# A seven-product group for the second retention pair, with banks, transposes and input chunks rearranged around it

## The chip, the cores and the metric

The kernel runs on one core of one Trainium2 chip. Its engines work from queues of their own: TensorE (PE in the profile) multiplies matrices, VectorE (DVE), ScalarE (ACT) and GpSimd (POOL) work on tiles, and SyncE (SP) issues most of the loads. The metric is device time in microseconds (us) for one execution; lower is better. Before the change the median of three runs is 1776.27 us (1775.71 to 1776.57).

## The reference

Two layers of a decoder trunk over 512 tokens with 1024 features, in float32. One projection feeds two branches, retention and an mLSTM; their gated sum goes through an output projection, a layer norm, a SwiGLU block and a second norm.

```python
proj = x @ w_in[l]
(r_q, r_k, r_v, r_g, m_qk, m_v, m_o, m_i, m_f, g_a, g_b) = jnp.split(proj, IN_OFFSETS, axis=-1)
rq = _rotary(r_q...);  rk = _rotary(r_k...) * (RET_QK_DIM ** -0.5)
o_ret = _head_norm(_retention(rq, rk, rv), ret_norm_g[l]) * silu(r_g)
mq, mk = silu(causal_conv(m_qk)) ...
o_ml = _head_norm(_mlstm(mq, mk, mv, i_pre, f_pre), mlstm_norm_g[l]) * sigmoid(m_o)
mix = (sigmoid(g_a) * (o_ret @ w_ret) + sigmoid(g_b) * (o_ml @ w_ml)) @ w_out[l]
x = layer_norm(alpha * x + mix);  x = layer_norm(alpha * x + swiglu(x))
```

Each branch has four heads, with 128 features for queries and keys and 256 for values.

## The kernel before, in words

**Precision.** Each float32 operand of a large product is split into a high part of a reduced type (`hi`, a cast on ScalarE, line 201) and the low rest (`lo`, a subtraction on VectorE, line 133). Each product is then three matmuls: high by high, high by low, low by high.

**Weights.** All weights lie in one array of units of 128 x 1024 values (512 KB). `layer_plan` lists a layer's units in the order of use. SP loads them into five raw buffers; `hi_to` and `prep_to` make the parts, up to five units ahead of use and four asked for by `used`. TensorE and SP follow the order in which the program is written out. The other engines are ordered by a planner, except inside the seven-product groups, where ScalarE, VectorE and GpSimd follow the program as well.

**Ways of multiplying.** `feat` (lines 266 to 268) takes one unit and makes 128 features for all 512 tokens, 24 matmuls of 512 columns. `tok_units` (lines 360 to 362) makes, over four units, 512 features for four blocks of 128 tokens, each in its own PSUM bank: a stream. `quad` (line 324) takes four units at once as a 2 x 2 block product and does it with seven block products instead of eight, 168 matmuls of 256 columns. It needs sums of weight blocks (`sum_to` line 191 on VectorE, line 223 on GpSimd) and sums of input blocks, the tiles `xs`, which `input_sums` makes (adds on GpSimd, line 589, four additions on VectorE, line 595, a cast on ScalarE, line 596, a low part on VectorE). Before the change, the mLSTM's queries and keys, the merge gates and most of the SwiGLU projections are made by such groups. Which units they take stands in `QUADS`.

**Banks.** PSUM has eight banks: four main ones (`main_bank`, `pm`), for units and streams, and four auxiliary ones (`aux_bank`, `pa`), for the side work. A group uses four main banks and one auxiliary one.

**Stages around the change.** For each retention pair `p` of two heads: four query/key units with the rotary turn (`rot_evac`, lines 618 to 621), for the first pair the gate unit (`feat_if`, whose `if_evac` is a chain of small operations on the rows of the input and forget gates), then a value stream and a gate stream. Then each mLSTM pair: a group with a convolution, a value stream, a gate stream.

**Side work and places.** The work of the heads is written as generators in the queue `side`; `slot()` takes one step of the first one in it. `slot()` is called after each token block of a stream (16 places a stream), after every two k-steps of a unit (4 places), and twice per block product of a group (14). `rest(n)` is `n` empty steps. The generators: `scores` (3 steps: two halves of the scores, lines 468 and 469; then key transposes, line 478, from which ScalarE and VectorE make the weighted keys, lines 482 and 483), `if_cols` (transposes of the gate rows, line 671), `weighted` (5 steps: the state, then four token blocks, lines 494 to 496), and `head_norms` (15 steps with 16 transposes, line 550). At the end of a pair, `drain()` runs what is left in the queue. A second queue, `slow`, holds `input_sums`; every fifth call of `slot()` (`SLOW`) takes one step of it. It is filled when the second retention pair starts.

The order in `side` for the first retention pair is: `scores` of the first head, `rest(12)`, `if_cols`; and, once the value stream has been written out, `weighted` of the first head, `scores` of the second, `rest(2)`, `weighted` of the second.

**The start.** The input comes transposed in six chunks (four of one k-tile, two of two), the first four units in matching pieces on SP's queue. The first four chunks are issued from ScalarE's queue, the last two from SP's, between the pieces. Each chunk is split (lines 428 to 433) when it lands. `first_units` multiplies the first four k-tiles for all four units, then the rest unit by unit (lines 343 to 345).

Of the kernel before, what the change touches and what calls it, by code (L numbers as in the profile page):

```python
# [10 lines left out]
F32 = mybir.dt.float32  # L11
F32R = mybir.dt.float32r
AF = mybir.ActivationFunctionType
ALU = mybir.AluOpType
# [84 lines left out]
QUADS = [layer_plan().index(("F", w, c + j * P)) for w, c, js in (("in", O_MQK, (0, 2)), ("in", O_GA, (0, 4)),  # L99
# [5 lines left out]
def decoder_trunk(ctx: ExitStack, tc: tile.TileContext, wall, xT_in, x_in, pvec, lnp, rtab, out):  # L105
# [15 lines left out]
    def aux_bank():  # L121
        return psa.tile([P, 512], F32, tag="a", name="pa")

# [119 lines left out]
    SLOW = 5  # L243
    turn = {"n": 0}

    def slot():
        turn["n"] += 1
        if slow and turn["n"] % SLOW == 0:
            if next(slow[0], "end") == "end":
                slow.popleft()  # L250
# [169 lines left out]
    k0 = 0  # L420
    for n in (1, 1, 1, 1, 2, 2):
        t = scratch([P, n, S], "xraw")
        ks, cs = slice(k0, k0 + n), slice(k0 * P, (k0 + n) * P)
        (nc.scalar if n == 1 else nc.sync).dma_start(t, xT_in[:, ks, :])
        for i, (r, hi, lo) in enumerate(firsts):
            nc.sync.dma_start(r[:, cs], wall[i][:, cs])
        if k0 == 0:
            nc.vector.tensor_copy(xh[:, ks, :], t)
        else:
            nc.scalar.copy(xh[:, ks, :], t)  # L430
        lo_of(xl[:, ks, :], t, xh[:, ks, :])
        for r, hi, lo in firsts:
            nc.scalar.copy(hi[:, cs], r[:, cs])
            lo_of(lo[:, cs], r[:, cs], hi[:, cs])
        k0 += n
# [23 lines left out]
    def scores(qk, hh, box, mult, key_weight, query_weight):  # L459
# [16 lines left out]
        pa = aux_bank()  # L476
# [21 lines left out]
    def weighted(box, vh, vl, hh, nv, done):  # L498
# [4 lines left out]
        pa = aux_bank()  # L503
# [6 lines left out]
        for i in range(NB):  # L510
            c, e = i // 2, i % 2
            pa = aux_bank()
            w = [(0, e * P)] + ([(1, HC)] if e else [])
            for n, (j, o) in enumerate(w):
                three(pa[:, :nv], cut(2 * c * W1 + o, P, W1), val(2 * c + j), n == 0, c == 0 and n == e)
            if c:
                three(pa[:, :nv], cut(O_QD + e * P, P, HC), st, False, True)
            done(i, pa)
            yield

    def head_norms(oo, p, gt, gain, od):
# [22 lines left out]
        for hh in range(2):  # L544
            m = 2 * (2 * p + hh)
            t = scratch([P, 2, S], "ot")
            for f in range(2):
                pa = aux_bank()
# [55 lines left out]
    for l in range(L):  # L604
# [9 lines left out]

        def rot_evac(dst):
            def ev(pm):
                t = scratch([P, S], "rt")
                nc.vector.tensor_tensor(out=dst, in0=pm, in1=tab[:, 0], op=ALU.mult)
                nc.vector.tensor_tensor(out=t[0:64], in0=pm[64:128], in1=tab[0:64, 1], op=ALU.mult)
                nc.vector.tensor_tensor(out=t[64:128], in0=pm[0:64], in1=tab[64:128, 1], op=ALU.mult)  # L620
                nc.gpsimd.tensor_tensor(out=dst, in0=dst, in1=t, op=ALU.add)
            return ev
# [44 lines left out]
        def if_cols():  # L667
            r3 = rows[:, 3]
            pa = aux_bank()
# [6 lines left out]
        for p in range(2):  # L676
            if p == 1:
                slow.append(input_sums(xh, xl, *xs))
# [30 lines left out]
            if p == 0:  # L709
                side.append(rest(12))  # L710
# [9 lines left out]
            tok_units([main_bank() for _ in range(NB)], lambda k: xh[:, k], lambda k: xl[:, k], K8, True, True, v_evac)  # L720
# [37 lines left out]
        def conv_ev(qk):  # L758
            t = {}
            part = lambda i, h: qk[:, 2 * i : 2 * i + 2, h * HC : (h + 1) * HC]  # L760
            two = lambda bank: bank.rearrange("p (j t) -> p j t", j=2)

            def ev(name, banks):
                if name == "p1":
                    t["u"] = scratch([P, 2, 2, HC], "mu")
                    nc.scalar.copy(t["u"][:, 0], two(banks["a"]))
                elif name == "p5":
                    nc.scalar.copy(t["u"][:, 1], two(banks["c"]))
                elif name == "p7":
                    nc.vector.tensor_tensor(out=part(1, 1), in0=t["u"][:, 1], in1=two(banks["d"]), op=ALU.subtract)  # L770
                elif name == "p6":
                    u, v = t["u"][:, 0], t["u"][:, 1]
                    nc.vector.tensor_tensor(out=u, in0=two(banks["b"]), in1=u, op=ALU.add)
                    nc.gpsimd.tensor_tensor(out=v, in0=v, in1=u, op=ALU.subtract)
                    nc.gpsimd.tensor_tensor(out=part(1, 1), in0=part(1, 1), in1=u, op=ALU.subtract)
                elif name == "p2":
                    nc.scalar.copy(part(0, 0), two(banks["a"]))
                    nc.vector.tensor_tensor(out=part(1, 0), in0=two(banks["e"]), in1=t["u"][:, 1], op=ALU.add)
                elif name == "p4":
                    nc.vector.tensor_tensor(out=part(0, 1), in0=two(banks["d"]), in1=t["u"][:, 0], op=ALU.add)  # L780
            return ev

        for p in range(2):
            qk = reg.tile([P, 4, S], F32, tag="qk", name="mqk")
            with tc.manual_schedule(engines=ordered):
                quad(xh, xl, *xs, conv_ev(qk))
# [42 lines left out]
            tok_units([main_bank() for _ in range(NB)], lambda k: xh[:, k], lambda k: xl[:, k], K8, True, True, v_evac)  # L829
# [22 lines left out]
            tok_units([main_bank() for _ in range(NB)], lambda k: xh[:, k], lambda k: xl[:, k], K8, True, True, g_evac)  # L852
            drain()
            gain = pv[:, C_MG : C_MG + 8]
# [379 lines left out]
```

## Time and profile before

| what | value |
|---|---|
| median of three runs | 1776.27 us (1775.71 to 1776.57) |
| profiled execution, its own time | 1776.88 us |
| span of the profile | 1775.2 us |
| TensorE busy | 1760.3 us, 99% |
| VectorE busy | 1311.3 us, 74% |
| ScalarE busy | 793.9 us, 45% |
| GpSimd busy | 432.9 us, 24% |
| mean granted TensorE clock | 0.998 |

The span runs from the first to the last instruction; the profiled execution's own time lies 1.7 us above it. Matmuls are pipelined: one of 512 columns is shown as some 0.39 us long, but the next starts 0.23 us after it, so starts are to be compared, not lengths. A row of a table of stretches gives the stretch, its length, the busy time of TensorE, its weight loads, VectorE, ScalarE and GpSimd with the number of instructions in brackets, the granted clock, the busy share of the DMA engines and what they moved in GB/s. A row of the time line gives start, length, engine, line, operation, output and inputs, shapes and count, and in brackets the idle time ahead with what ended it.

### The profile page before, as it was taken

Reading aid. Unit: us, or ns where it says so; the run is one execution under the profiler, and the core shown is the slowest. Engines: PE = TensorE matmul, PEld = TensorE weight load, DVE = VectorE, ACT = ScalarE, POOL = GpSimd, SP = SyncE. Lnnn points to the kernel's source line nnn. Section 1 sums busy time; section 2 is a strip of 40 time slices with the busy share of each in tenths; the row PEclk is TensorE's granted clock in tenths of the full one; section 3 lists DMA queues with packets and bytes.
Section 4 is the critical chain, followed back from the end, with each engine's and each line's share of the span. In section 5 each row is a group of like instructions: output and inputs, shape, how many; then the busy total and the mean of one; then the engine's idle time right before and its main releaser. Section 6 shows DMA issues by size and latency. Waiting matters only on the chain.

```text
span 1775.2 us, 27167 instructions
## 1 busy us (share of the span) xinstructions
PE 1760.3 (99%) x10904; PEld 1586.0 (89%) x10904; DVE 1311.3 (74%) x1735; ACT 793.9 (45%) x1157; POOL 432.9 (24%) x321
## 2 busy tenths in 40 slices
PE   9999999999999999999999999999999999999997
PEld 7888898998889999988898898989988899999886
DVE  7686878795559999863476868787845699998534
ACT  5445555663226444451244455556533254445310
POOL 2141110231001555520121311112300115555200
PEclk9999999999999999999999999999999999999999
DMA  7222422346333333363243323313553223333521
GB/s 253 91 91 81 142 79 88 111 141 235 96 114 109 99 96 108 107 213 96 84 166 91 110 86 107 119 60 108 201 179 119 96 95 107 111 116 112 187 70 48
DMA packets 76174, 209.49 MB, mean 118 GB/s; under 512 B 6760, under 2 KB 9832, under 8 KB 75024
## 3 DMA queue, kind: packets, MB, share of 16 engines
q1 hardware_dynamic: 65632, 167.27, 29.5%
q0 software_dynamic: 9840, 39.43, 6.3%
q8 instruction: 86, 1.41, 0.3%
q10 hardware_dynamic: 576, 1.05, 0.2%
q14 instruction: 40, 0.33, 0.1%
HBM read 190.93 MB, written 16.79 MB: 117 GB/s over the span
## 4 chain that ended last, share of the span: by engine, by line
PE 97%; DVE 1%; DMA 1%; ACT 1%; issue 0%; SPq 0%; DVEq 0%
PE pm L324 31%; PE pm L360 9%; PE pm L362 9%; PE pm L361 9%; PE pm L267 5%; PE pm L266 5%; PE pm L268 5%; PE pa L324 5%; PE pa L361 3%; PE pa L360 3%; PE pa L362 3%; PE pa L494 1%; PE pa L495 1%; PE pa L496 1%; PE pa L550 1%; PE pa L468 1%
## 5 line engine op out<-in xcount | busy, mean ns | idle before, releaser
L133 DVE TENSOR_TENSOR wlo<-wraw,whi 128x1024 fp32r<-128x1024 f32 (+2 forms) x424 | 597.0, 1421 | 201.9 <-ACT whi L201 198.9
L201 ACT CAST whi<-wraw 128x1024 fp32r<-128x1024 f32 x402 | 419.9, 1049 | 471.0 <-PE pm L267 115.2
L450 POOL TENSOR_TENSOR rs<-ve,nhalf 128x4 f32<-128x4 f32 (+1 forms) x32 | 31.9, 997 | 482.6 <-DVE ve L449 482.6
L223 POOL TENSOR_TENSOR wraw<-wraw 128x1024 f32<-128x1024 f32 x32 | 77.0, 2406 | 151.2 <-issue 57.9
L360 PE MATMUL pm<-whi,x0h 128*128 128x512 f32 x256 | 102.9, 402 | 1.5 <-DVE rvl L133 1.5
L360 PE MATMUL pm<-whi,x20h 128*128 128x512 f32 x256 | 102.5, 400 | 0.6 <-DVE rvl L133 0.6
L362 PE MATMUL pm<-wlo,x0h 128*128 128x512 f32 x256 | 100.7, 393 | 0.0
L361 PE MATMUL pm<-whi,x0l 128*128 128x512 f32 x256 | 100.4, 392 | 0.0
L362 PE MATMUL pm<-wlo,x20h 128*128 128x512 f32 x256 | 100.3, 392 | 0.0
L361 PE MATMUL pm<-whi,x20l 128*128 128x512 f32 x256 | 100.1, 391 | 0.0
L1085 POOL TENSOR_TENSOR qa<-qa 128x512 f32<-128x512 f32 x20 | 42.8, 2141 | 142.6 <-DVE qa L1084 90.6
L324 PE MATMUL pm<-x10h,whi 128*128 128x256 f32 x240 | 67.9, 283 | 0.0
L324 PE MATMUL pm<-x10l,whi 128*128 128x256 f32 x240 | 67.9, 283 | 0.0
L324 PE MATMUL pm<-s0h,whi 128*128 128x256 f32 x240 | 67.9, 283 | 0.0
L324 PE MATMUL pm<-s0l,whi 128*128 128x256 f32 x240 | 67.9, 283 | 0.0
L324 PE MATMUL pm<-s0h,wlo 128*128 128x256 f32 x240 | 67.9, 283 | 0.0
L324 PE MATMUL pm<-x11h,whi 128*128 128x256 f32 x240 | 67.9, 283 | 0.0
L324 PE MATMUL pm<-x11l,whi 128*128 128x256 f32 x240 | 67.9, 283 | 0.0
L324 PE MATMUL pm<-x11h,wlo 128*128 128x256 f32 x240 | 67.9, 283 | 0.0
L324 PE MATMUL pm<-s1h,whi 128*128 128x256 f32 x240 | 67.9, 283 | 0.0
L324 PE MATMUL pm<-s1l,whi 128*128 128x256 f32 x240 | 67.9, 283 | 0.0
L324 PE MATMUL pm<-s1h,wlo 128*128 128x256 f32 x240 | 67.9, 283 | 0.0
(519 smaller groups left out, 5675.2 us busy)
## 6 DMA issues: line engine op xcount, KB each, us to landing
wraw<-wall SPq DMA_DIRECT2D x306, 512.0 KB, 3.8
od<-ot POOLq DMA_DIRECT2D x16, 512.0 KB, 3.6
of<-od POOLq DMA_DIRECT2D x16, 512.0 KB, 5.0
gb<-lnp POOLq DMA_DIRECT2D x4, 1024.0 KB, 6.2
x1d<-xr POOLq DMA_DIRECT2D x8, 512.0 KB, 2.9
xr<-x1d POOLq DMA_DIRECT2D x8, 512.0 KB, 4.8
negm<-md POOLq DMA_DIRECT2D x2, 1026.0 KB, 6.6
xr<-xtok POOLq DMA_DIRECT2D x4, 512.0 KB, 6.8
```

Source lines behind the costliest of these rows:

```text
L133: nc.vector.tensor_tensor(out=out_lo, in0=full, in1=hi.bitcast(F32), op=ALU.subtract)
L201: nc.scalar.copy(hi, sum_t[i])
L223: nc.gpsimd.tensor_tensor(out=raw_t[u + 2], in0=raw_t[u], in1=raw_t[u + 3], op=ALU.add)
L266: nc.tensor.matmul(pm[:, c0:c1], lhsT=hi[:, k], rhs=xh[:, k, c0:c1], start=(k == 0), stop=False)
L267: nc.tensor.matmul(pm[:, c0:c1], lhsT=hi[:, k], rhs=xl[:, k, c0:c1], start=False, stop=False)
L268: nc.tensor.matmul(pm[:, c0:c1], lhsT=lo[:, k], rhs=xh[:, k, c0:c1], start=False, stop=(k == KT - 1))
L324: nc.tensor.matmul(pm, lhsT=x[:, j, k], rhs=y[:, k], start=go and n == 0, stop=j == 1 and k == 3 and n == 2, skip_group_check=not first)
L360: nc.tensor.matmul(pm, lhsT=sh(k)[:, a], rhs=hi[:, j], start=first, stop=False)
L361: nc.tensor.matmul(pm, lhsT=sl(k)[:, a], rhs=hi[:, j], start=False, stop=False)
L362: nc.tensor.matmul(pm, lhsT=sh(k)[:, a], rhs=lo[:, j], start=False, stop=last)
L450: nc.gpsimd.tensor_tensor(out=rs[:, :n], in0=ve[:, :n], in1=nhalf[:, :n], op=ALU.pow)
L1085: nc.gpsimd.tensor_tensor(out=v, in0=v, in1=u, op=ALU.subtract)
```

## The change

- The four query/key units of the second retention pair become a group of seven products (`QUADS`, `quad`, with the mLSTM's evacuation `conv_ev` under the name `blocks_ev`). The rotary turn is then done in place on the evacuated tile (`rotate`).
- The input sums are put into `slow` right after the gate unit of the first pair, with `SLOW` 3 instead of 5, and what is left of them runs before the group.
- `if_cols` comes after `rest(20)` instead of `rest(12)`; the second pair has a `rest(7)` ahead of its first scores, as the mLSTM pairs do.
- The gate streams (swish gates and output gates) take the auxiliary banks, and the side work takes main banks while they run (`stream_banks`, `head_bank`).
- All six input chunks are issued first, from ScalarE's queue; the last two have a buffer of their own (`x_late`).

```diff
-QUADS = [... for w, c, js in (("in", O_MQK, (0, 2)), ("in", O_GA, (0, 4)),
+QUADS = [... for w, c, js in (("in", O_RQ, (2,)), ("in", O_MQK, (0, 2)), ("in", O_GA, (0, 4)),
...
+    turned = {"now": False}
+
+    def head_bank():
+        return main_bank() if turned["now"] else aux_bank()
+
+    def stream_banks(second):
+        turned["now"] = second
+        return [aux_bank() if second else main_bank() for _ in range(NB)]
...
-    SLOW = 5
+    SLOW = 3
...
-    for n in (1, 1, 1, 1, 2, 2):
-        t = scratch([P, n, S], "xraw")
+    x_late = reg.tile([P, 4, S], F32, tag="gt", name="x_late")
+    x_raw = [(k, 1, scratch([P, 1, S], "xraw")) for k in range(4)] + [(k, 2, x_late[:, k - 4 : k - 2]) for k in (4, 6)]
+    for k0, n, t in x_raw:
+        nc.scalar.dma_start(t, xT_in[:, k0 : k0 + n, :])
+    for k0, n, t in x_raw:
         ks, cs = slice(k0, k0 + n), slice(k0 * P, (k0 + n) * P)
-        (nc.scalar if n == 1 else nc.sync).dma_start(t, xT_in[:, ks, :])
...
-            pa = aux_bank()
+            pa = head_bank()
...
+        def rotate(dst, x):
+            t = scratch([P, S], "rt")
+            nc.vector.tensor_tensor(out=t[0:64], in0=x[64:128], in1=tab[0:64, 1], op=ALU.mult)
+            nc.vector.tensor_tensor(out=t[64:128], in0=x[0:64], in1=tab[64:128, 1], op=ALU.mult)
+            nc.vector.tensor_tensor(out=dst, in0=x, in1=tab[:, 0], op=ALU.mult)
+            nc.gpsimd.tensor_tensor(out=dst, in0=dst, in1=t, op=ALU.add)
...
         for p in range(2):
-            if p == 1:
-                slow.append(input_sums(xh, xl, *xs))
...
             else:
-                for ev in rots:
-                    feat(xh, xl, ev)
+                while slow:
+                    slow_step()
+                with tc.manual_schedule(engines=ordered):
+                    quad(xh, xl, *xs, blocks_ev(qk))
+                for i in range(4):
+                    rotate(qk[:, i], qk[:, i])
+                side.append(rest(7))
             if p == 0:
                 feat_if(xh, xl, if_evac)
+                slow.append(input_sums(xh, xl, *xs))
...
-                side.append(rest(12))
+                side.append(rest(20))
                 side.append(if_cols())
...
-            tok_units([main_bank() for _ in range(NB)], lambda k: xh[:, k], lambda k: xl[:, k], K8, True, True, g_evac)
+            tok_units(stream_banks(True), lambda k: xh[:, k], lambda k: xl[:, k], K8, True, True, g_evac)
             drain()
+            turned["now"] = False
```

More of the change, by code (lines that the diff above doesn't have):

```diff
@@ L98 @@
 NUNIT = len(layer_plan())
-QUADS = [layer_plan().index(("F", w, c + j * P)) for w, c, js in (("in", O_MQK, (0, 2)), ("in", O_GA, (0, 4)),
+QUADS = [layer_plan().index(("F", w, c + j * P)) for w, c, js in (("in", O_RQ, (2,)), ("in", O_MQK, (0, 2)), ("in", O_GA, (0, 4)),
                                                                   ("in", O_GB, (0, 4)), ("gu", 0, range(2, FT, 2))) for j in js]
@@ L242, in decoder_trunk, with slow_step @@
     side, slow = deque(), deque()
-    SLOW = 5
+    SLOW = 3
     turn = {"n": 0}
+    def slow_step():
+        if next(slow[0], "end") == "end":
+            slow.popleft()
     def slot():
@@ L248, in slot @@
         if slow and turn["n"] % SLOW == 0:
-            if next(slow[0], "end") == "end":
-                slow.popleft()
+            slow_step()
         while side:
@@ L434, in decoder_trunk @@
             lo_of(lo[:, cs], r[:, cs], hi[:, cs])
-        k0 += n
     for i, (r, hi, lo) in enumerate(firsts):
@@ L475, in scores @@
             yield
-        pa = aux_bank()
+        pa = head_bank()
         for j in range(2):
@@ L502, in weighted @@
         val = lambda j: (vh[:, j, hh, :], vl[:, j, hh, :])
-        pa = aux_bank()
+        pa = head_bank()
         for j in range(2):
@@ L511, in weighted @@
             c, e = i // 2, i % 2
-            pa = aux_bank()
+            pa = head_bank()
             w = [(0, e * P)] + ([(1, HC)] if e else [])
@@ L547, in head_norms @@
             for f in range(2):
-                pa = aux_bank()
+                pa = head_bank()
                 for b in range(NB):
@@ L613, in decoder_trunk, with blocks_ev, ev @@
         od = [dr.tile([P, KT, S], F32, tag=f"od{i}", name="od") for i in range(2)]
-        def rot_evac(dst):
[L616 to L622, printed above, removed]
+        def blocks_ev(qk):
+            t = {}
+            part = lambda i, h: qk[:, 2 * i : 2 * i + 2, h * HC : (h + 1) * HC]
+            two = lambda bank: bank.rearrange("p (j t) -> p j t", j=2)
+            def ev(name, banks):
+                if name == "p1":
+                    t["u"] = scratch([P, 2, 2, HC], "mu")
+                    nc.scalar.copy(t["u"][:, 0], two(banks["a"]))
+                elif name == "p5":
+                    nc.scalar.copy(t["u"][:, 1], two(banks["c"]))
+                elif name == "p7":
+                    nc.vector.tensor_tensor(out=part(1, 1), in0=t["u"][:, 1], in1=two(banks["d"]), op=ALU.subtract)
+                elif name == "p6":
+                    u, v = t["u"][:, 0], t["u"][:, 1]
+                    nc.vector.tensor_tensor(out=u, in0=two(banks["b"]), in1=u, op=ALU.add)
+                    nc.gpsimd.tensor_tensor(out=v, in0=v, in1=u, op=ALU.subtract)
+                    nc.gpsimd.tensor_tensor(out=part(1, 1), in0=part(1, 1), in1=u, op=ALU.subtract)
+                elif name == "p2":
+                    nc.scalar.copy(part(0, 0), two(banks["a"]))
+                    nc.vector.tensor_tensor(out=part(1, 0), in0=two(banks["e"]), in1=t["u"][:, 1], op=ALU.add)
+                elif name == "p4":
+                    nc.vector.tensor_tensor(out=part(0, 1), in0=two(banks["d"]), in1=t["u"][:, 0], op=ALU.add)
+            return ev
@@ L668, in if_cols @@
             r3 = rows[:, 3]
-            pa = aux_bank()
+            pa = head_bank()
             for b in range(NB):
@@ L718, in v_evac @@
                 lo_of(vl[:, b], src, vh[:, b])
-            tok_units([main_bank() for _ in range(NB)], lambda k: xh[:, k], lambda k: xl[:, k], K8, True, True, v_evac)
+            tok_units(stream_banks(False), lambda k: xh[:, k], lambda k: xl[:, k], K8, True, True, v_evac)
             oo = reg.tile([P, 2, NB, DV], F32, tag="oo", name="roo")
@@ L756, in conv @@
             nc.scalar.activation(x, t, AF.Silu)
[L758 to L781, printed above, removed]
         for p in range(2):
@@ L785, in decoder_trunk @@
             with tc.manual_schedule(engines=ordered):
-                quad(xh, xl, *xs, conv_ev(qk))
+                quad(xh, xl, *xs, blocks_ev(qk))
             for i in range(4):
@@ L827, in v_evac @@
                 lo_of(vl[:, b, :, :DV], src, vh[:, b, :, :DV])
-            tok_units([main_bank() for _ in range(NB)], lambda k: xh[:, k], lambda k: xl[:, k], K8, True, True, v_evac)
+            tok_units(stream_banks(False), lambda k: xh[:, k], lambda k: xl[:, k], K8, True, True, v_evac)
             oo = reg.tile([P, 2, NB, DV], F32, tag="oo", name="moo")
@@ L850, in g_evac @@
                 nc.scalar.activation(gt[:, b], pm, AF.Sigmoid)
-            tok_units([main_bank() for _ in range(NB)], lambda k: xh[:, k], lambda k: xl[:, k], K8, True, True, g_evac)
+            tok_units(stream_banks(True), lambda k: xh[:, k], lambda k: xl[:, k], K8, True, True, g_evac)
             drain()
+            turned["now"] = False
             gain = pv[:, C_MG : C_MG + 8]
```

3 lines of the change are left out of this document (2 added, 1 removed).

## The prediction

> **What bounds the kernel now.** I read the page first, then TensorE's waits, then busy time in stretches cut at the first matmul of each stage.
>
> ```profile
> span 1775.2 us, 27167 instructions
> PE 1760.3 (99%) x10904; PEld 1586.0 (89%) x10904; DVE 1311.3 (74%) x1735; ACT 793.9 (45%) x1157; POOL 432.9 (24%) x321
> PE 97%; DVE 1%; DMA 1%; ACT 1%; issue 0%; SPq 0%; DVEq 0%
> ```
>
> TensorE is busy for 99% of the span and is 97% of the chain that ended last. Only two things move the time: fewer TensorE cycles, or the places where TensorE stands or runs slowly. The profiled execution took 1776.88 us (span 1775.2 and 1.7 around it), 0.6 above the median of 1776.27; differences are worked out in the trace and taken off the median.
>
> The waits of TensorE (line, what for, us in total, times, longest):
>
> ```profile
> PE pm L360 <- DVE rvl L133: 2.0, 2, 1.5
> PE pm L344 <- DVE wlo L133: 1.6, 2, 0.8
> ```
>
> Stretches (us, busy time and count of each engine, granted clock, DMA): the four first units; layer 0's first retention pair, value and gate streams; the second pair's four query/key units; its streams; the first mLSTM group of seven products; layer 1's first-pair streams.
>
> ```profile
> 5.00:30.71 25.71, 23.84 (x97) 17.88 (x97) 18.32 (x41) 13.26 (x32) 3.44 (x3) 1.00 0.91 314
> 34.33:92.27 57.94, 56.47 (x278) 47.58 (x276) 40.87 (x78) 27.39 (x47) 7.25 (x6) 0.97 0.34 102
> 92.27:115.93 23.66, 23.66 (x113) 19.60 (x112) 17.63 (x27) 10.59 (x16) 10.81 (x8) 1.00 0.34 103
> 115.93:170.19 54.26, 54.26 (x274) 46.08 (x272) 40.60 (x69) 24.91 (x43) 11.99 (x10) 1.00 0.25 82
> 170.19:191.99 21.80, 21.80 (x185) 21.80 (x184) 14.99 (x20) 14.31 (x22) 4.13 (x4) 1.00 0.51 160
> 916.09:971.60 55.51, 54.94 (x278) 46.32 (x276) 39.04 (x75) 28.57 (x48) 7.10 (x6) 1.00 0.30 91
> ```
>
> **The group of seven products (gain 3.7).** The four units take 23.66 us with 112 weight loads: 96 matmuls of 512 columns and 16 head-norm transposes. The existing mLSTM group does the same algebra on the same shapes in 21.80 us: 168 matmuls of 256 columns and the same 16 transposes. The new group also has 14 slots with a head norm queued in them, so I take that row over: 23.66 - 21.80 = 1.86 a layer, 3.7 in both. Its three more operands (casts, low parts, block sums) are hidden as there: in the 21.80 row VectorE works 14.99, ScalarE 14.31, and TensorE all of it. The same four 512 KB loads arrive. If that cover were gone, the units of the first row above show the price: a wait per operand.
>
> The 12 rotary passes and four GpSimd adds now run after the group instead of between units. The first head's two need, with the rows below, 6 x 0.69 and a 2.3 us add, 6.5 us; the scores that read them come after one leftover head-norm step and the seven empty places of `rest(7)`, about nine blocks of six matmuls (1.36 us each, from the 0.227 spacing below), 12 us. I cost this at nothing.
>
> ```profile
> L618 DVE TENSOR_TENSOR rqk<-pm,rtab x16: 682/688/692, 22.7 to 995.5; 128x512 f32<-128x512 f32 x16
> L621 POOL TENSOR_TENSOR rqk<-rqk,rt x16: 1287/2308/2334, 24.9 to 997.7; 128x512 f32<-128x512 f32 x16
> ```
>
> **Banks traded, transposes later (gain 4.3).** At the end of the first pair's value stream:
>
> ```profile
> 57.77 0.44 PE L671 MATMUL pa<-ident,rows 36*128 36x36 f32 x4
> 58.96 1.87 DVE L133 TENSOR_TENSOR rvl<-pm,rvh 128x512 fp32r<-128x512 f32 x3
> 59.68 0.50 PE L360 MATMUL pm<-whi,x0h 128*128 128x512 f32 x1 [1.47 <-DVE rvl L133]
> 60.00:62.00 2.00, 2.00 (x7) 1.55 (x6) 2.00 (x4) 0.21 (x1) 0.00 (x0) 0.57 0.83 248
> 62.00:64.00 2.00, 2.00 (x10) 1.86 (x9) 0.90 (x3) 0.37 (x1) 0.00 (x0) 0.58 0.46 90
> 939.53 0.44 PE L671 MATMUL pa<-ident,rows 36*128 36x36 f32 x4
> 940.54 0.50 PE L360 MATMUL pm<-whi,x20h 128*128 128x512 f32 x1 [0.57 <-DVE rvl L133]
> ```
>
> The gate stream waits for its first main bank, which VectorE empties late because the gate-row chain holds it; after 1.47 us of idling the granted clock is 0.57 for some 4 us. With the auxiliary banks this stream needs nothing of that. Against the second pair's 54.26 us the first pairs are 3.68 and 1.25 longer; I leave 0.3 each for the four transposes, which stay: 3.4 + 0.95 = 4.3. Lower bound 3.3, if the transposes stall at their new place.
>
> That can happen: the input sums come from the second pair into these streams (`SLOW` 3, appended after `feat_if`).
>
> ```profile
> L595 DVE TENSOR_TENSOR sf<-xs 128x256 f32<-128x256 f32 x16 | 11.7, 760 | 1.3 <-POOL rqk L621 1.2
> L595 DVE TENSOR_TENSOR sf<-sf,xs 128x256 f32<-128x256 f32 x16 | 6.6, 417 | 0.1
> L133 DVE TENSOR_TENSOR xs0l<-sf,xs0h 128x1024 fp32r<-128x1024 f32 x4 | 5.1, 1269 | 1.6 <-ACT xs0h L596 1.6
> ```
>
> For one layer (11.7 + 6.6)/2 + 5.1 = 14.2 us on top of VectorE's 40.87 in 57.94: nearly full. TensorE has weights some four units ahead, and eight places are about 11 us of slack, so I take no loss; bound 0 to 3.4 a layer, the stall just shown.
>
> **Input chunks first (gain 2.0).** In the first units, from the fourth chunk on:
>
> ```profile
> 15.29 0.39 PE L345 MATMUL pm<-x0l,whi 128*128 128x512 f32 x1
> 16.65 0.39 PE L345 MATMUL pm<-x0l,whi 128*128 128x512 f32 x1
> 18.55 0.50 PE L344 MATMUL pm<-x0h,wlo 128*128 128x512 f32 x1 [0.80 <-DVE wlo L133]
> 21.29 0.50 PE L344 MATMUL pm<-x0h,wlo 128*128 128x512 f32 x1 [0.79 <-DVE wlo L133]
> 21.63 0.40 PE L345 MATMUL pm<-x0l,whi 128*128 128x512 f32 x1
> 6.00:8.00 2.00, 2.00 (x9) 1.50 (x10) 0.75 (x3) 1.32 (x5) 0.00 (x0) 1.00 0.61 168
> 8.00:10.00 2.00, 2.00 (x10) 1.45 (x9) 2.00 (x7) 1.72 (x7) 0.00 (x0) 1.00 0.58 160
> L424 ACTq DMA_DIRECT2D xraw<-xt x4: 335/428/453, 0.8 to 8.7; - x4
> 2.21 1.28 ACT L433 ACT_TABLE_LOAD   x1 [2.21 <-issue]
> 4.17 0.30 ACT L433 CAST whi<-wraw 128x128 fp32r<-128x128 f32 x1 [0.69 <-DMA wraw<-wall]
> ```
>
> Six matmuls from 15.29 take 1.36, 0.227 each. From 16.65 to 21.63 nine start, 2.04 us of work in 4.98: 2.9 lost to the last two chunks and their weights. The DMA engines are only 0.6 busy from 6 to 10, so earlier chunks have room. Against it: six issues of 0.43 from 0.81 end at 3.4, the table load behind them at 4.7, so the first cast is 0.5 later than 4.17; and the weight pieces on SP's queue share the engines with 2 MB of chunks. I take 2.0; bounds -1 (early weights late, no gain) and 2.9.
>
> **What the later transposes push out (loss 9.2).** Places are counted in the code: a stream gives 16, one after each token block. Before: scores of the first head at 1 to 3, 12 empty ones, transposes at 16, then in the gate stream five weighted steps, three scores, two empty ones, five weighted steps: place 31 of 32. With `rest(20)` the transposes are at 24, the first weighted steps at 25 to 29, the second head's scores at 30 to 32, and its five weighted steps fall into `drain()`, with no stream matmul between them; the queue is one line, so nothing passes. TensorE goes in program order, so the whole new group waits behind them. The first weighted step reads the key weights, made by ScalarE and VectorE (L482, L483, twice) from the transposes at place 32:
>
> ```profile
> 77.36 0.38 PE L478 MATMUL pa<-ident,rqk 128*128 128x128 f32 x2
> 80.94 0.35 DVE L483 SCALAR_TENSOR_TENSOR pp<-pa,pv,pp 128x128 fp32r<-128x128 f32 x1 [0.43 <-ACT pp L482]
> 90.76 0.28 PE L496 MATMUL pa<-pp 128*128 128x256 f32 x1
> 208.42 0.38 PE L478 MATMUL pa<-ident,mqk 128*128 128x128 f32 x2
> 210.53 0.35 DVE L483 SCALAR_TENSOR_TENSOR pp<-pa,kw,pp 128x128 fp32r<-128x128 f32 x1
> 39.77 0.38 PE L478 MATMUL pa<-ident,rqk 128*128 128x128 f32 x2
> 47.98 0.35 DVE L483 SCALAR_TENSOR_TENSOR pp<-pa,pv,pp 128x128 fp32r<-128x128 f32 x1
> ```
>
> Now this takes 3.9 us under the gate stream (77.36 to 81.29, the same head), 2.5 at best (208.42 to 210.88), 8.6 where VectorE is crowded (39.77 to 48.33); all of it is covered now, the last weighted step ending 1.5 us before the stream. Uncovered, TensorE idles for that less the transposes (0.38) and the three products of the first key weight (about 0.36): 3.2, 1.8 or 7.8. I take 2.9, near the same head's row, since nothing new comes from TensorE meanwhile. That is more than the 1.47 that cost the clock, so I add 4 us at 0.575, 1.7. Each drain 4.6, both layers 9.2. The later steps find their operands: five steps give each other cover, and their banks are the main ones.
>
> Here the Trainium skill would have it otherwise. TensorE: Matmul & The Clock Gate, Part 1: The HAM clock gate, says that the clock falls to half after an idle window of about 3.4 us. The trace disagrees: it shows 0.57 after 1.47 us, so the measurement decides; by the rule the drains would be 3.4 us cheaper together.
>
> **Sum:** 3.7 + 4.3 + 2.0 - 9.2 = 0.8, so 1776.27 - 0.8 = **1775.5**, no change: within 0.2% (3.55 us, about what a measurement of this kernel can tell), 1772.7 to 1779.8.
>
> **Rivals.** *The clock holds in the drains.* For it: layer 1's 0.57 us of idling left the clock at 1.00 in its row of stretches; against it, 2.9 us is twice layer 0's 1.47. Loss 2 x 2.9: 1776.27 - 10.0 + 5.8 = 1772.1, faster.
> *The key weights are made at once.* For it: 2.5 us at 208.42, and the streams' work ends there; against it, the gate evictions and next casts are queued at the same moment. 1.8 idle, no clock loss: 1776.27 - 10.0 + 3.6 = 1769.9, faster.
> *The key weights stand behind a crowd, slower.* One mechanism, in both drains: 14.2 us of sums push VectorE's other work to the stream's end. For it: the 8.6 us row, where VectorE was crowded; against it, the sums' last step is at place 22, ten before. Idle 7.8 and 1.7 each: 1776.27 - 10.0 + 19.0 = 1785.3. It decides from 6.8 a drain, (10.0 + 3.55)/2, which is 5.8 us for the key weights.
> *The chunks bring nothing* because the weights come later by as much: 1777.5, still no change.
>
> **Chances.** Forecast, with the idle start in it, 0.40; clock holds 0.22; key weights at once 0.13; crowd 0.25. So faster 0.35, same 0.40, slower 0.25. The range: from the at-once case less part of the start's 0.9 in reserve, 1769.3, to a crowd of about 8 a drain, 1776.27 - 10.0 + 16 = 1782.3, rounded to 1782.5; the far crowd and a bad start lie outside. The likeliest case's own range is 1772.7 to 1779.8.
>
> **What would show it.** The second pair's group at 21.8 us, no wait of the first pair's gate stream on `rvl`, TensorE's ninth matmul after the fourth chunk by about 19 us instead of 21.6; and between the first pair's last gate matmul and the group, five weighted steps in a row behind a wait on L483, with the clock under 1 after it. I am wrong if that wait is under 1 us or over 5, if the clock stays at 1.00, or if TensorE stands at the transposes' new place.

## The result: slower by 8.7 us

The changed kernel takes 1784.98 us (median; 1784.45 to 1787.31) beside 1776.25 (1774.56 to 1777.58) for the kernel before, a ratio of 1.0053 with an interval of 1.0042 to 1.0064. The forecast was 1775.5 with a range to 1782.5, so the kernel came out slower, 2.5 us beyond the range. Code lines of the changed kernel lie some 11 to 50 further down than those of before; the names are the same.

The page of the kernel after (span; busy time, share and instructions of each engine; the chain that ended last, by engine):

```profile
span 1784.0 us, 27496 instructions
PE 1759.2 (99%) x11048; PEld 1594.0 (89%) x11048; DVE 1330.5 (75%) x1755; ACT 800.3 (45%) x1169; POOL 458.9 (26%) x327
PE 93%; DVE 4%; DMA 1%; ACT 1%; issue 1%; SPq 0%; DVEq 0%; ACTq 0%
```

The span grew by 8.8. VectorE holds 4% of the chain instead of 1%: TensorE now stands for it. TensorE's longest waits after (what, for what, us in total, times, longest):

```profile
PE pm L357 <- ACT whi L448: 4.5, 1, 4.5
PE pm L509 <- DVE pp L144: 3.7, 2, 1.8
PE pm L508 <- DVE cols L712: 2.8, 2, 1.8
PE pm L508 <- ACT pp L496: 2.3, 4, 0.7
```

The last three are new, and the wait of the gate stream on `rvl` is gone. The stretches after, cut as before: first units; layer 0's first-pair streams; the new group; layer 1's first-pair streams; its group.

```profile
9.37:32.67 23.30, 23.30 (x96) 19.24 (x97) 17.55 (x38) 13.29 (x32) 2.08 (x2) 0.94 0.91 318
36.30:99.50 63.20, 57.80 (x278) 47.76 (x276) 53.45 (x94) 30.52 (x48) 23.70 (x14) 0.97 0.18 59
99.50:121.28 21.78, 21.78 (x186) 21.78 (x185) 15.78 (x23) 13.18 (x21) 5.04 (x4) 1.00 0.54 159
921.11:982.68 61.57, 57.55 (x277) 47.83 (x276) 51.66 (x91) 31.79 (x49) 25.09 (x13) 0.97 0.17 55
982.68:1004.48 21.80, 21.80 (x187) 21.80 (x185) 15.78 (x23) 13.17 (x21) 5.02 (x4) 1.00 0.56 163
```

| stretch | after less before, us |
|---|---|
| end of the first units (32.67 against 30.71) | +2.0 |
| first-pair streams, layer 0 (63.20 against 57.94) | +5.3 |
| first-pair streams, layer 1 (61.57 against 55.51) | +6.1 |
| group in place of four units, both layers | -3.75 |
| second-pair streams, both layers (54.38 against 54.26 in layer 0) | +0.2 |
| all else | -0.9 |

The loss lies in the first-pair streams, where VectorE's busy time went from 40.87 to 53.45 us and GpSimd's from 7.25 to 23.70: the input sums. TensorE's time line there, after, layer 0 (71.50 is the four gate-row transposes in their new place, L508 to L510 a weighted step, three matmuls to each product):

```profile
71.50 0.44 PE L711 MATMUL pm<-ident,rows 36*128 36x36 f32 x4
...
81.27 0.36 PE L508 MATMUL pm<-rvh,pp 128*128 128x256 f32 x1 [1.76 <-DVE cols L712]
83.91 0.50 PE L509 MATMUL pm<-pp 128*128 128x256 f32 x1 [1.84 <-DVE pp L144]
...
94.84 0.39 PE L508 MATMUL pm<-rvh,pp 128*128 128x256 f32 x1 [0.73 <-ACT pp L496]
96.04 0.39 PE L508 MATMUL pm<-rvh,pp 128*128 128x256 f32 x1 [0.43 <-ACT pp L496]
```

TensorE idles 3.6 us in the middle of the gate stream, and only 1.2 in the drain. The first of these waits is for `cols`, VectorE's copy of the transposed gate rows (L712). The bank written at 81.27 is a main one, as was that of the transposes. In between, the weighted steps took three more main banks (from 73.36, 75.48 and 77.24), and there are four. The trace doesn't number the banks, but by this count the side work, which takes main banks now, had come round to the bank that the copy had still to empty. The next wait is for the low part of the state. VectorE and then ScalarE at that time, after:

```profile
79.69 1.22 DVE L144 TENSOR_TENSOR xs0l<-sf,xs0h 128x1024 fp32r<-128x1024 f32 x1
80.83 0.30 DVE L712 COPY cols<-pm 128x144 f32<-128x144 f32 x1
81.04 1.22 DVE L144 TENSOR_TENSOR wlo<-wraw,whi 128x1024 fp32r<-128x1024 f32 x1
82.29 1.23 DVE L202 TENSOR_TENSOR wraw<-wraw 128x1024 f32<-128x1024 f32 x1
83.44 0.42 DVE L144 TENSOR_TENSOR pp<-pm,pp 128x256 fp32r<-128x256 f32 x1
81.16 0.22 ACT L713 ACTIVATE en<-cols 128x16 f32<-128x16 f32 x1 [1.62 <-DVE cols L712]
81.28 0.35 ACT L521 CAST pp<-pm 128x256 fp32r<-128x256 f32 x1
```

The transposes that the copy reads ended near 72; the copy ran at 80.83. VectorE's rows follow each other without a gap; directly ahead of the copy stands a low part of the input sums, and between it and the low part that TensorE wants (83.44) stand two weight operations of 1.2 us each. ScalarE, in order too, waits for the copy (L713) with the state's cast behind it. The clock after it, in stretches of two us:

```profile
84.00:86.00 2.00, 2.00 (x6) 1.71 (x7) 1.93 (x6) 1.32 (x2) 0.00 (x0) 0.50 0.67 195
86.00:88.00 2.00, 2.00 (x10) 1.71 (x10) 0.57 (x3) 0.94 (x2) 1.87 (x1) 0.64 0.21 76
94.00:96.00 2.00, 0.88 (x5) 0.49 (x3) 0.99 (x3) 1.99 (x5) 0.00 (x0) 1.00 0.01 4
```

After the stall in the gate stream it is 0.50, at the drain 1.00.

At the start, the issues on ScalarE's queue after, and VectorE's first cast, which waits for the first chunk:

```profile
4.35 0.33 ACTq L437 DMA_DIRECT2D xraw<-xt  x1
5.46 0.34 ACTq L437 DMA_DIRECT2D x_late<-xt  x1
7.36 0.33 ACTq L437 DMA_DIRECT2D x_late<-xt  x1
7.72 1.28 ACT L448 ACT_TABLE_LOAD   x1 [7.72 <-DMA xraw<-xt]
9.02 0.89 ACT L448 CAST whi<-wraw 128x128 fp32r<-128x128 f32 x4
4.35 0.43 DVE L443 CAST x0h<-xraw 128x512 fp32r<-128x512 f32 x1 [3.27 <-DMA xraw<-xt]
```

The fourth issue starts at 4.35, in the moment the first chunk has landed; the fifth and sixth follow 1.1 and 3.0 us later. The table load, at 2.21 before, and the first weight casts stand behind the sixth. So TensorE starts at 9.37 instead of 5.00. It then needs 23.30 us instead of 25.71 for the first units.

### The profile page after: what moved, and what is told of

It is laid out like the page before. It is cut to its first block, busy times and chain, and to the rows that moved or that the text cites. A ratio compares the mean times of both kernels' runs of the same rounds, so it can differ in the third digit from the quotient of the medians.

```text
span 1784.0 us, 27496 instructions
## 1 busy us (share of the span) xinstructions
PE 1759.2 (99%) x11048; PEld 1594.0 (89%) x11048; DVE 1330.5 (75%) x1755; ACT 800.3 (45%) x1169; POOL 458.9 (26%) x327
## 4 chain that ended last, share of the span: by engine, by line
PE 93%; DVE 4%; DMA 1%; ACT 1%; issue 1%; SPq 0%; DVEq 0%; ACTq 0%
PE pm L338 33%; PE pa L376 6%; PE pa L375 6%; PE pa L374 6%; PE pm L374 6%; PE pm L376 6%; PE pm L375 6%; PE pa L338 5%; PE pm L280 4%; PE pm L282 4%; PE pm L281 4%; DVE wlo L144 1%; DMA wraw<-wall 1%; PE pm L509 1%; PE pm L508 1%; PE pm L510 1%
## 5 line engine op out<-in xcount | busy, mean ns | idle before, releaser
L144 DVE TENSOR_TENSOR wlo<-wraw,whi 128x1024 fp32r<-128x1024 f32 (+2 forms) x430 | 606.6, 1424 | 209.3 <-ACT whi L212 203.6
L212 ACT CAST whi<-wraw 128x1024 fp32r<-128x1024 f32 x408 | 426.1, 1049 | 471.3 <-PE pm L281 108.9
L234 POOL TENSOR_TENSOR wraw<-wraw 128x1024 f32<-128x1024 f32 x34 | 81.7, 2403 | 180.2 <-issue 57.9
L338 PE MATMUL pm<-x10h,wlo 128*128 128x256 f32 x240 | 68.0, 283 | 0.0
L202 DVE TENSOR_TENSOR wraw<-wraw 128x1024 f32<-128x1024 f32 x34 | 52.3, 1539 | 0.1
L374 PE MATMUL pm<-whi,x0h 128*128 128x512 f32 x128 | 51.2, 400 | 0.6 <-DVE rows L680 0.6
L374 PE MATMUL pa<-whi,x0h 128*128 128x512 f32 x128 | 51.8, 405 | 0.0
L374 PE MATMUL pa<-whi,x20h 128*128 128x512 f32 x128 | 51.6, 403 | 0.0
L374 PE MATMUL pm<-whi,x20h 128*128 128x512 f32 x128 | 51.2, 400 | 0.0
```

The source lines that it names most:

```text
L144: nc.vector.tensor_tensor(out=out_lo, in0=full, in1=hi.bitcast(F32), op=ALU.subtract)
L202: nc.vector.tensor_tensor(out=f, in0=f, in1=e, op=ALU.add)
L212: nc.scalar.copy(hi, sum_t[i])
L234: nc.gpsimd.tensor_tensor(out=raw_t[u + 2], in0=raw_t[u], in1=raw_t[u + 3], op=ALU.add)
L338: nc.tensor.matmul(pm, lhsT=x[:, j, k], rhs=y[:, k], start=go and n == 0, stop=j == 1 and k == 3 and n == 2, skip_group_check=not first)
L374: nc.tensor.matmul(pm, lhsT=sh(k)[:, a], rhs=hi[:, j], start=first, stop=False)
```

## The experiments

Two theories stood against each other from the beginning. **Crowd:** the input sums in the first pair's streams hold VectorE up, and TensorE with it. **Drain:** the later place of the transposes pushes the second head's weighted steps out of the streams, as forecast, and its price is higher than forecast. Times are medians; each ratio is against the kernel before in the same comparison (1775.49 to 1776.23).

### The parts alone: start, and banks

*The start alone*, in the kernel before:

```diff
+    x_late = reg.tile([P, 4, S], F32, tag="gt", name="x_late")
...
+    for k0, n, t in x_raw:
+        nc.scalar.dma_start(t, xT_in[:, k0 : k0 + n, :])
...
-        (nc.scalar if n == 1 else nc.sync).dma_start(t, xT_in[:, ks, :])
```

> The kernel before with the six input chunks first, nothing else changed. If ScalarE's queue is what is late (theory): its first cast moves from 4.2 to about 9 us, the first four units end 2.0 us later (about 32.7 instead of 30.7), and the whole takes about 1778.2. If the start only looks late because of what follows (rival, the prediction's term): the units end about 2.0 earlier and the whole takes about 1774.3.

Measured: 1776.87, ratio 1.0005 (0.9995 to 1.0014). The first units end at 33.33, 2.6 later than before, but layer 0's first-pair streams then take 56.68 instead of 57.94. TensorE stands in them for as long as before (1.5 us, of which 1.28 at the bank), but this time its clock stays at 1.00 afterwards. The end moves by no more than can be told from nothing. The start is worth about nothing, neither the gain of 2.0 nor the 2.0 to 2.6 us that its own stage shows.

*The banks alone*, in the kernel before, transposes where they were:

```diff
-            pa = aux_bank()
+            pa = head_bank()
...
-            tok_units([main_bank() for _ in range(NB)], ..., g_evac)
+            tok_units(stream_banks(True), ..., g_evac)
```

> The kernel before with the banks traded, transposes still after 12 empty places. If the gate stream only waited for a main bank (theory): the first pair's streams take about 54.6 us in both layers instead of 57.9 and 55.5, the whole about 1772. If the gate-row chain or the copy of the transposes' bank is next in line (rival): the wait moves to the transposes or to the weighted steps that need their bank, and the whole stays within 1774 to 1777.

Measured: 1773.02, ratio 0.9985 (0.9976 to 0.9995): faster than both kernels. The first-pair streams of the two layers:

```profile
33.99:89.12 55.13, 55.13 (x278) 46.30 (x276) 40.78 (x78) 27.32 (x47) 7.26 (x6) 1.00 0.36 107
912.94:967.80 54.86, 54.86 (x277) 46.31 (x276) 39.04 (x75) 28.60 (x48) 7.12 (x6) 1.00 0.30 92
```

57.94 became 55.13 and 55.51 became 54.86, together 3.46 shorter; TensorE is busy all the time at a clock of 1.00. What follows is compared with these two numbers, 109.99 us in sum; the changed kernel has 124.77, 14.8 more.

*Another way to bring the last chunks early*, with the banks traded: the fifth and sixth chunk in `x_late`, issued on SP's queue ahead of the third and fourth weight pieces, nothing more on ScalarE's.

```diff
-        (nc.scalar if n == 1 else nc.sync).dma_start(t, xT_in[:, ks, :])
+        if n == 1:
+            nc.scalar.dma_start(t, xT_in[:, ks, :])
+        if k0 in (2, 3):
+            j, m, u = x_raw[k0 + 2]
+            nc.sync.dma_start(u, xT_in[:, j : j + m, :])
```

> The kernel before with banks traded and the last two input chunks in a buffer of their own, issued from SP's queue ahead of the weight pieces of the third and fourth k-tile; the first four chunks stay on ScalarE's queue as before. If the late chunks cost the 2.9 us after the fourth k-tile (theory): the first four units end about 2 us earlier than the 30.4 of the run with banks only, the whole is about 1771. If the weight pieces become late by as much (rival): 30.4 and 1773.

Measured: 1772.98, ratio 0.9985 (0.9976 to 0.9994), the same as with the banks alone. The first units end at 31.17 instead of 30.36: the waits for weight parts only move, from between 16.9 and 20.9 us to between 11.9 and 17.7.

### Taking parts out of the changed kernel

*The old start:*

```diff
-    for k0, n, t in x_raw:
-        nc.scalar.dma_start(t, xT_in[:, k0 : k0 + n, :])
...
+        (nc.scalar if n == 1 else nc.sync).dma_start(t, xT_in[:, ks, :])
```

> The changed kernel with the old order of the input chunks. If the start is a loss of its own (theory): the first matmul is at 5.0 again, the first four units end at about 30.7, the whole is about 2.0 us faster than the changed kernel, 1783. If the late start had given the first pair's streams slack that is now gone (rival): their waits grow by as much and the whole stays at 1785.

Measured: 1784.79, ratio 1.0050 (1.0033 to 1.0067). The first units end at 30.50 again, and the time stays within 0.2 us of that of the changed kernel. The start isn't the cause.

*No group:* four units again, the sums back in the second pair; the banks, `rest(20)` and the start stay.

```diff
-    SLOW = 3
+    SLOW = 5
...
+            if p == 1:
+                slow.append(input_sums(xh, xl, *xs))
...
-                    quad(xh, xl, *xs, blocks_ev(qk))
...
+                for ev in rots:
+                    feat(xh, xl, ev)
```

> The changed kernel without the group and with the input sums back in the second pair (every fifth place); banks, transposes after 20 places and early chunks stay. If the sums on VectorE make the wait in the first pair's gate stream (crowd theory): no wait on the copy of the gate columns, the first pair's streams take about 56 us (54.6 and some 1.3 in the drain) instead of 63.2 and 61.6, the whole about 1776.5. If the bank that the transposes share with the weighted steps makes it (bank theory), or the later place does: the waits of about 1.8 and 1.8 us with the lower clock stay, and the whole is about 1787.

Measured: 1787.12, ratio 1.0062 (1.0047 to 1.0077). The crowd theory alone falls here: with no sums in the first pair the kernel isn't faster. TensorE's waits of this kernel that bear on it:

```profile
PE pm L508 <- ACT pp L496: 5.0, 4, 1.9
PE pm L510 <- DVE pp L497: 1.0, 2, 0.5
```

The waits on `cols` and on the state's low part are gone, and the waits for the key weights, in the drain, have grown from 2.3 to 6.0 in both layers. So there are two losses, and each shows when the other is away.

*The drain taken out of the changed kernel:* no `drain()` after the first pair, no `rest(7)`, so the leftover steps go under the group.

```diff
-                side.append(rest(7))
...
-            drain()
+            if p == 1:
+                drain()
```

> The changed kernel without the drain behind the first pair's gate stream and without the seven empty places of the second pair: the last five weighted steps fall into the group's places. Crowd theory: only the waits in the drain go, 1.3 us a layer, as the waits on the gate columns and on the state's low part stand in the gate stream before it: about 1782.5. If the drain is the main loss (the prediction's term): 4.6 a layer, about 1776.

Measured: 1784.62, ratio 1.0050 (1.0035 to 1.0065). The waits of the drain are gone, those on `cols` (2.2) and the state's low part (3.7) stay, and nothing measurable is won. In the changed kernel the waits of the drain aren't what costs.

*The transposes back at `rest(12)`, in the changed kernel:*

```diff
-                side.append(rest(20))
+                side.append(rest(12))
```

> The changed kernel with the transposes back at place 16 (12 empty places). If only the place makes the loss (place theory): the weighted steps all fit into the gate stream, the first pair's streams take about 54.6 us each, the whole about 1770. If VectorE is too full for the early place (crowd theory): the transposes wait some 3 us for the gate rows (their last copy ends at 63.6 in the changed kernel, the place is at about 60.3), then the first weighted step waits for the value low parts, with the clock down after it; the streams stay near 63 us and the whole near 1785.

Measured: 1788.32, ratio 1.0071 (1.0056 to 1.0086), slower than the changed kernel by about 3.3 us. TensorE's waits:

```profile
PE pa L711 <- DVE rows L702: 5.2, 2, 3.1
PE pm L508 <- DVE rvl L144: 4.7, 2, 3.4
```

With the sums in these streams the gate-row chain (`rows`) and the values' low parts (`rvl`) come late, and TensorE meets them earlier. The later place is a gain as long as the sums are there.

### Adding parts to the banks alone

*The later place alone:* banks traded and `rest(20)`, nothing else.

```diff
-                side.append(rest(12))
+                side.append(rest(20))
```

> The kernel before with banks traded, and the transposes after 20 empty places instead of 12, nothing else: the price of the later place without sums and without the group. From the run without the group: some 3 us of waiting on the key weights in each drain and the low clock behind it, first-pair streams about 61.7 instead of 55, the whole about 1786. If that loss came from the early chunks (rival): 1773.

Measured: 1785.04, ratio 1.0051 (1.0036 to 1.0066), 12.0 slower than the banks alone (+8.8 against -3.2). A row each of this kernel's stretches, its time line and its stretches of two us, at layer 0's drain:

```profile
34.28:94.73 60.45, 57.13 (x278) 47.92 (x276) 41.53 (x76) 28.82 (x48) 6.94 (x6) 0.97 0.34 105
87.36 0.39 PE L503 MATMUL pm<-rvh,pp 128*128 128x256 f32 x1 [1.86 <-ACT pp L491]
90.00:92.00 2.00, 1.79 (x8) 1.79 (x9) 0.71 (x3) 0.74 (x2) 0.00 (x0) 0.52 0.58 127
```

This is the forecast's drain: five weighted steps in a row, an idle start for the key weights, then half the clock. It costs 5.3 us in layer 0 (60.45 less 55.13) and 5.5 in layer 1, where 4.6 each was forecast.

*The sums alone:* banks traded, the sums in the first pair with `SLOW` 3, four units, `rest(12)`, the old start.

```diff
-    SLOW = 5
+    SLOW = 3
...
-            if p == 1:
-                slow.append(input_sums(xh, xl, *xs))
...
+                slow.append(input_sums(xh, xl, *xs))
```

> The kernel before with banks traded and the input sums made in the first pair (every third place), no group, transposes at place 16, old start. The price of the sums alone against the run with banks only (1773.0). Crowd theory: the first pair's streams rise from 55 to about 62 us by waits on the gate rows and on the value low parts, and the sums leave the second pair: about 1786. If the sums are hidden (the prediction's reading, no loss): 1773.

Measured: 1788.78, ratio 1.0074 (1.0057 to 1.0091), 15.8 slower than the banks alone by the two medians. The streams take 62.68 and 62.60, 15.3 more in sum. Its waits are those of the run with `rest(12)` above, longer for `rows` (7.2) and shorter for `rvl` (2.9). Five rows of its time line, in order of time:

```profile
54.65 4.44 POOL L598 TENSOR_TENSOR xs<-x0h,x0l 128x512 f32<-128x512 f32 x1 [6.44 <-DVE sf L604]
57.87 1.23 DVE L669 TENSOR_TENSOR mp<-rows 4x1 f32<-4x1 f32 x1
59.93 2.54 POOL L598 TENSOR_TENSOR xs<-x0h,x0l 128x512 f32<-128x512 f32 x1
61.38 1.37 DVE L671 COPY rows<-rows 4x512 f32<-4x512 f32 x1
62.81 0.42 PE L680 MATMUL pa<-ident,rows 36*128 36x36 f32 x2 [4.21 <-DVE rows L671]
```

An addition of four numbers takes VectorE 1.23 us and ends at 59.10, with GpSimd's addition of 128x512 (59.09). The copy of four rows takes 1.37 and ends 0.3 after the next one of GpSimd. TensorE stands for this chain.

*The sums without GpSimd's additions:* the block sums are made of the high parts alone.

```diff
-            t = scratch([P, 2, S], "xs")
-            for i in range(2):
-                nc.gpsimd.tensor_tensor(out=t[:, i], in0=xh..., in1=xl..., op=ALU.add)
+            t = xh.bitcast(F32)[:, m : m + 5 : 4]
```

> The run with early sums and no group (1788.8), with GpSimd's 8 additions of high and low input parts a layer left out: the sums are taken of the high parts alone, so the low part of the input is missing from them. If VectorE's own 14.2 us a layer make the crowd (theory): the waits on the gate rows and value low parts shrink by less than a third, 1784 to 1789. If VectorE's small operations were mainly held up beside GpSimd's additions (rival: a row copy of 0.42 us took 1.37 beside one): about 1776 to 1780.

Measured: 1780.79, ratio 1.0027 (1.0017 to 1.0037). The same two operations of VectorE, and the stretch of layer 0's first-pair streams:

```profile
56.84 0.14 DVE L667 TENSOR_TENSOR mp<-rows 4x1 f32<-4x1 f32 x1
59.26 0.42 DVE L669 COPY rows<-rows 4x512 f32<-4x512 f32 x1
34.50:93.13 58.63, 55.42 (x277) 46.30 (x276) 48.93 (x98) 30.67 (x51) 4.42 (x4) 1.00 0.32 101
```

They are back at 0.14 and 0.42 us. VectorE's 98 instructions in this stretch are busy for 48.93 us; with GpSimd's additions its 98 instructions in the same stretch were busy for 53.64. In sum the streams take 118.91 (60.28 in layer 1), 6.4 less than with GpSimd's additions and 8.9 more than with the banks alone; by the medians against the kernel before, 8.7 of 16.5 us go with the additions. So about half of the sums' price (42% by the one, 53% by the other) goes with GpSimd's additions, the rest with the sums' other work. How that rest divides wasn't measured.

### Two ways round that didn't work

*The gate rows in the second pair*, so that only the sums are added to the first (old start):

```diff
-        if p == 0:
+        if p == 1:
             feat("if", 0)
...
-            if p == 0:
                 feat_if(xh, xl, if_evac)
+            if p == 0:
                 slow.append(input_sums(xh, xl, *xs))
...
-            if p == 0:
-                side.append(rest(20))
+            if p == 1:
+                side.append(rest(6))
```

> The changed kernel with the old start and with the gate unit, its chain of small operations and the transposes moved from the first retention pair to the second, behind the group; the sums stay in the first pair, whose weighted steps start with its gate stream again, so nothing is left for the drain. Crowd theory: with the chain (some 12 us of VectorE) in the second pair, which has lost the sums, both pairs have room; all four stretches of streams take 54 to 55 us, the group saves its 1.9 us a layer, and the whole is about 1769.5, faster than banks alone (1773.0). If the sums by themselves are too much for the first pair (rival): waits on the value low parts stay there and the whole is 1775 to 1785.

Measured: 1805.43, ratio 1.0166 (1.0151 to 1.0181); the expectation fell. TensorE's waits:

```profile
PE pm L374 <- DVE rows L682: 15.8, 2, 7.9
PE pm L508 <- DVE rvl L144: 9.7, 2, 5.1
```

The second is the crowd without the gate-row chain: the first pair's streams still take 63.17 in layer 0, now standing for the values' low parts. The first wait was made by the edit itself, at the gate unit in its new place, so the whole time says nothing on the sums.

*The sums queued behind the value stream*, every second place, with `rest(12)` and the old start:

```diff
-    SLOW = 3
+    SLOW = 2
...
-                side.append(rest(20))
+                side.append(rest(12))
...
+            if p == 0:
+                slow.append(input_sums(xh, xl, *xs))
```

> The changed kernel with the old start, the transposes at place 16 again, and the input sums put into the queue only behind the first pair's value stream, a step at every second place of its gate stream. If the crowd is one of the value stream alone, where the gate-row chain, the value low parts and the sums meet (theory): the waits on the gate rows and the value low parts go, the group keeps its 1.9 us a layer, and the whole is 1769 to 1772, faster than banks alone. If VectorE has no room in the gate stream either, or the planner pulls the additions forward again (rival): 4 to 8 us of waits a layer, 1777 to 1785.

Measured: 1783.33, ratio 1.0041 (1.0027 to 1.0056). TensorE still waits, for the weighted keys (4.7 in both layers) and for the gate rows (3.6). The planner had drawn GpSimd's first additions forward to 37.98, into the value stream, so the sums weren't kept out of it.

## Why the prediction was wrong

| term | forecast | measured |
|---|---|---|
| group of seven products | 3.7 gain | 3.75 gain in its stretches |
| banks traded | 4.3 gain, transposes later | 3.2 gain, transposes left in place |
| input chunks first | 2.0 gain | 0.2 to 0.65 loss, not told from nothing |
| drains | 9.2 loss | 12.0 loss by themselves, hardly any beside the sums |
| sums in the first-pair streams | 0, bound 3.4 a layer | 15.3 loss by itself, 7.6 a layer |
| drains and sums together, in the first-pair streams | 9.2 loss | 14.8 loss |

**The step that failed** is "TensorE has weights some four units ahead, and eight places are about 11 us of slack, so I take no loss". By themselves the sums cost 7.6 us a layer, over twice the upper bound. In the changed kernel TensorE's waits for VectorE in the gate stream, where no loss was taken, come to 6.5 us over both layers; those in the drains, where the loss was put, come to 2.3. The slack was counted from the weights and the transposes, but VectorE works in order: the copy of the gate rows, the values' low parts and the state's low part all stand behind the sums, and each has TensorE or ScalarE waiting. The amount of work wasn't the mistake: 40.87 + 14.2 is 55.1, and VectorE was busy for 53.45. But this room is that of the whole stretch, while each operand is wanted at a place within it. And beside GpSimd's additions single operations of VectorE take longer: in the changed kernel a scan in the gate-row chain (L697) took 1.78 us instead of 0.74 and the operation after it (L701) 1.77 instead of 0.68; in the run with the sums alone it was 1.23 instead of 0.14 and 1.37 instead of 0.42. The bound of 3.4 came from the one stall shown before, which had another cause.

**The sums are not the one cause.** The four combinations, all with the banks traded (medians, us):

| | transposes after 12 empty places | after 20 |
|---|---|---|
| sums in the second pair | 1773.02 | 1785.04 |
| sums in the first pair | 1788.78 | 1784.79, with the group |

Each of the two moves costs 12 to 16 us alone, and both together cost no more than the sums do: 1784.79 with the group's 3.75 put back is 1788.5. So taking out one of them doesn't bring the time back. Without the sums the kernel took 1787.12; less the 3.75 of the group, as an estimate, that is 1783.4, still just beyond the range, because the drain's price was too small as well and the start brought nothing. Forecast and result are 9.5 us apart. In the trace, 6.4 of this lie in the first-pair streams (4.9 longer forecast, 11.3 measured) and 4.0 at the end of the first units (2.0 earlier forecast, 2.0 later measured); the rest of the kernel takes 0.7 less than forecast.

The Trainium skill has the mechanism: SBUF — State Buffer, in the section on the two separate sides, says that a GpSimd instruction that reads SBUF and a VectorE instruction with two inputs there, or in a two-port mode, need the same port pair, that whichever starts first holds it under an exclusive lock for its whole length, and that the other is blocked. The time line agrees: the addition of four numbers ends 0.01 us from the end of GpSimd's. That it is this lock is the page's reading; the runs show that the time goes with GpSimd's additions. I hadn't weighed it.

**The drain** was right as a mechanism and somewhat small: 5.3 and 5.5 us a layer, with five weighted steps in a row, 3.2 us of idling in layer 0 (1.86 and two shorter waits), and a clock of 0.52 behind it, against 4.6 forecast. Here the row decided rightly against the rule of the Trainium skill cited there (TensorE: Matmul & The Clock Gate, Part 1: The HAM clock gate): the clock fell although the longest idle time was 1.86 us. But the forecast summed its terms, and the losses don't add: by themselves 15.3 for the sums and 10.8 for the later place in these streams, together 14.8. Where TensorE has stood for VectorE in the gate stream, the second head's key weights come nearly in time, with 1.2 us of idling in the drain, and its clock stays at 1.00. By the marks that I set for it the step is wrong in the changed kernel: the clock stays at 1.00, and the first wait is 0.73 us, under the 1 us that was set (1.2 with the second).

**The group** saves what its row said, in both layers, and its rotary turn costs nothing. **The banks** were forecast a quarter too high: the streams got 2.81 and 0.65 shorter, where 3.4 and 0.95 stood. **The start:** the forecast had "six issues of 0.43 from 0.81 end at 3.4"; they end at 7.7: the fourth starts only when the first chunk has landed, and the table load and the first casts stand behind the sixth. The ninth matmul after the fourth chunk, my sign for this step, now follows without a wait, 2.04 us behind, but at 23.6 instead of 19: 2.4 us are saved inside the first units and 4.4 lost ahead of them. Of the 2.0 that remain, the old start wins back only 0.2 of the whole time.

**The rivals.** The slower one, 1785.3, has the time, and its "crowd" is what TensorE waits for in the changed kernel; but it placed the crowd at the key weights in the drains, 7.8 us of idling there, where there are 1.2. I argued against it that "the sums' last step is at place 22"; but the sums did their damage at operands that TensorE reads ahead of the drain. That the clock holds in the drains came true in the changed kernel, with no gain in it; that the chunks bring nothing holds.

The best version is the banks alone, 1773.02 us, 0.9985 (0.9976 to 0.9995). Whether the sums can be put anywhere ahead of the group for less than the 3.7 us that it saves stays open: each place tried here costs more.

## What to carry to other kernels

Before work is moved under a stream, count the room of each side engine in that stretch, in order and not as a mean: which operands of the stream stand behind the moved work, and which engine shares its way to memory. Stalls in one line of work aren't additive, in either direction: a part that costs 12 us alone can be free, or even a gain, beside another that costs 15, so parts are to be timed alone before the change is put together. And issues of DMAs on an engine that also computes can hold its work back: here the sixth came at 7.36, and the first weight casts behind it.

## What was not expected of the hardware

- VectorE beside GpSimd: a 4x1 addition of 0.14 us takes 1.23, a 4x512 copy of 0.42 takes 1.37, each ending with GpSimd's addition or 0.3 us after it.
- Of six issues on ScalarE's queue, the fourth starts at 4.35, when the first chunk has landed, and the sixth at 7.36. The first three had gone out at once; whether the chip or the program's waits hold the others, no run here told apart.
- The clock went to 0.50 after two idle times of 1.76 and 1.84 us with a short run of matmuls between them, and to 0.52 after 1.86, 0.63 and 0.75; after 0.73 and 0.43 it stayed at 1.00. But the length of the idle times alone doesn't decide. In the run with the sums queued behind the value stream, both layers have the same two waits at the weighted keys, 0.33 and 2.35 us; after them the clock is 0.50 in layer 0 (from 86 to 88 us) and 1.00 in layer 1 (from 970 to 972). And with the start alone it stayed at 1.00 after 1.28, where 1.47 had cost it before. What else decides, no run here shows; so the 1.7 us that the forecast added to each drain for the clock were not certain either.
